# First loads in another order and in smaller pieces, and a last norm with other steps, in a one-core decoder layer

## The chip, the core and the metric

The kernel runs on one core of a Trainium2 chip. The metric is the device time of one execution in microseconds; three executions were timed and their median is given. One more execution was recorded by the hardware profiler. TensorE (PE) multiplies matrices, VectorE (DVE) and ScalarE (ACT) work on elements, GpSimd (POOL) too; loads and stores are issued from the queues of SyncE (SP), ScalarE and GpSimd and carried by 16 DMA engines.

## The reference

One layer of a hybrid decoder, over 512 prompt tokens and 8 x 8 sample tokens, 576 columns in all. Two branches, an RWKV-7 state scan and a differential attention, read the same normalised input; gates merge them, an MLP with squared ReLU follows, and a final RMSNorm.

```
def rmsnorm(x, g, eps):
    y = x * lax.rsqrt(jnp.mean(x * x, axis=-1, keepdims=True) + eps)
    return y * g

xn = rmsnorm(x, g_mix, 1e-6)
P = xn @ w_in                      # 1024 -> 1792 + 1536 + 2048 columns
o_a, S = rwkv7_branch(P[:1792], ...)
o_b = attend(q, k, v from P[1792:3328], ...)
m = sigmoid(P[3328:4352]) * (o_a @ w_br_a) + sigmoid(P[4352:]) * (o_b @ w_br_b)
x = x + m @ w_out
hn = rmsnorm(x, g_ffn, 1e-6)
x = x + square(relu(hn @ w_up)) @ w_down
y = rmsnorm(x, g_final, 1e-6)
```

All tensors are float32. The kernel lays features on the 128 partitions and tokens along the columns: x is eight tiles (k-tiles) of 128 features by 576 tokens.

## The kernel before

Every product of two float32 matrices is made of three products. An operand is split into a rounded high half and the rest (`hi` by ScalarE, line 58; `lo` by VectorE, line 61), and hi x hi, hi x lo and lo x hi are added up in one PSUM bank (`stream`, lines 158 to 201). A weight tile goes through three steps for that: load, `hi`, `lo`.

The kernel does not write the order of its instructions down. Each gets a priority (`prio`, a lower number is earlier), and a scheduler places the instructions of each engine by priority and by the time at which it thinks that their inputs are there. `FEED` is for loads and halves, `FILL` for matmuls; without either the place in the program counts. Eight semaphores serve the loads of SP's and ScalarE's queues in turn, so a load that takes one up again waits until the last transfer on it has landed.

The start: line 111 loads `vec`, all per-channel vectors (67 columns, 33.5 KB), and line 113 `cst`, the masks and the identity (374 KB), both from ScalarE's queue. Lines 275 to 291 load the eight tiles of x (288 KB each) and the first weights of q, k and v in pieces of four k-tiles (256 KB) from SP's queue. Then `xh` is x scaled by a column of `vec` and rounded, `xl` the rest (lines 297 and 298). The first norm's squares are summed beside it (`acc`), and its factor R1 is multiplied in later. `qkv(0)` multiplies the k-tiles for q, k and v in turn, each with two halves of 288 tokens. Nine products of a constant tile warm TensorE up (`warmup`).

The second norm (from line 1280): `colsum` sums the squares `acc` over the partitions on TensorE, one column a group of tokens; from it come M2 and R2 = 1/m, for the columns of all tokens. The MLP's input is not scaled by M2, so its result must be scaled: the residual is multiplied by M2 when the first product is added, and the last sum by R2.

The final norm: the last down products are made for 320 tokens first and 256 after (`LAST`). For each of the eight output tiles, `ev` adds the product to the residual (`fin`), scales it by R2, and squares it. The squares of seven tiles are added to `acc`; those of the last one are summed apart (`last`). Two column sums, one power (GpSimd, line 1351), and transposes that spread the factor over the partitions (`pb`) follow; ScalarE copies the factor to SBUF as R3 for GpSimd. VectorE multiplies six output tiles from the bank `pb`, GpSimd two (1 and 4) from R3, and four stores write them, ending after tiles 1, 3, 5 and 8 (`ends`), from SP and ScalarE in turn.

Of the kernel before, what the change touches and what calls it, by code (L numbers as in the profile page):

```python
# [8 lines left out]
F32 = mybir.dt.float32  # L9
# [6 lines left out]
P = 128  # L16
D = 1024
# [24 lines left out]
def tile_hybrid_step(ctx, tc, xT, xsT, ktab, vtab, s0T, ptab, w_in, vecs, w2a2, g2, lamv,  # L42
# [70 lines left out]
    nc.scalar.dma_start(out=c, in_=cst)  # L113
# [20 lines left out]
    def v(i, n=1):  # L134
        return vec[:, i:i + n]
# [18 lines left out]
    def stream(src, kt, xh, xl, spans, evac, name, raws=None, together=False, banks=None,  # L154
# [12 lines left out]

        def halve(i):
            raw = raws[i]
            with prio(FEED + 1000 * job + 100 if banks is None else FEED + 1001 + 40 * i + job):  # L170
                if keep:
                    hi, lo = (t[:, i * n:(i + 1) * n] for t in keep)
                elif banks is None or i == 0:
                    hi = ring["pool"].tile([P, n, P], F32R, tag="hi", name=f"hi_{name}_{i}")
                    lo = ring["pool"].tile([P, n, P], F32R, tag="lo", name=f"lo_{name}_{i}")
                else:
# [4 lines left out]
                his.extend(hi[:, k] for k in range(n))  # L181
                los.extend(lo[:, k] for k in range(n))
# [88 lines left out]
    with tc.tile_pool(name="xin", bufs=2, reuse_waits="tile") as xin:  # L271
        xt = [xin.tile([P, NT], F32, name=f"x{k}", bufs=1) for k in range(KT)]
        xs_ = xin.tile([P, KT, NB], F32, name="xs", bufs=1)
        acc = xin.tile([P, NT], F32, name="acc", bufs=1)
        with prio(FEED):
            nc.sync.dma_start(out=xt[0], in_=xT[:, 0])
        first = [(j + 1, []) for j in range(3)]
        for k in range(0, KT, 4):
            for j in range(3):
                with prio(FEED + 1000 + 10 * k + j):  # L280
                    name = f"raw_{'qkv'[j]}0_{k}"
                    if k == 0:
                        raw = ring["pool"].tile([P, 4, P], F32, tag="raw", name=name, bufs=3)
                    else:
                        raw = zw.tile([P, 1 + NX], F32, tag="z" if j else "tz", name=name,
                                      bufs=2 if j else 1)[:, :4 * P].rearrange("p (k w) -> p k w", k=4)
                    ring["dma"] = nc.sync.dma_start(out=raw, in_=w_in[14 + 4 * j][:, k:k + 4])
                    first[j][1].append(raw)
            with prio(FEED + 1005 + 10 * k):
                for i in range(max(k, 1), k + 4):  # L290
                    nc.sync.dma_start(out=xt[i], in_=xT[:, i])
# [3 lines left out]
        for k in range(KT):  # L295
            with prio(FEED + 1000 + 10 * k):
                act(xh[:, k, :NT], xt[k], scale=v(V_GM + k))
                stt(xl[:, k, :NT], xt[k], v(V_GM + k), f32(xh[:, k, :NT]), MUL, SUB)
# [869 lines left out]
    ends = (1, 3, 5, 8)  # L1168
# [5 lines left out]
    qs = {}  # L1174

# [308 lines left out]
```

## Time and profile before

| | |
|---|---|
| median of three executions | 1007.83 us (1004.7 to 1008.62) |
| the profiled execution | 1006.88 us, its span 1005.1 us |
| TensorE busy | 975.1 us, 97% of the span |
| VectorE, ScalarE, GpSimd busy | 688.9, 497.0, 87.5 us |
| DMA | 105.75 MB, 105 GB/s in the mean |

The span is what the profiler saw from the first instruction to the last; the execution's own time is 1.8 us more. Busy times overlap. The chain of waits follows the work that ended last back to its start, each time to what released it, and so shows which engine's time counts at which place.

### The profile page before, as it was taken

What the parts mean: (1) busy time and instruction counts of PE and PEld (TensorE: products, weight loads), DVE (VectorE), ACT (ScalarE), POOL (GpSimd) and SP (SyncE); (2) the same over time, 40 slices, a digit from 0 to 9 for tenths busy, and PEclk for the clock granted to TensorE, in tenths of its full rate; (3) what the DMA queues carried; (4) which work ended last, traced back from release to release, by engine and by line L of the source; (5) the groups of instructions that cost most, each with busy time, mean ns of one, the idle gap of its engine ahead of it and who ended that gap; (6) DMA issues with size and microseconds to landing.
All of it is one profiled execution on the core that took longest, in us unless ns stands there. A gap on an engine that the chain in (4) does not pass through costs nothing.

```text
span 1005.1 us, 24415 instructions
## 1 busy us (share of the span) xinstructions
PE 975.1 (97%) x10012; PEld 919.4 (91%) x10012; DVE 688.9 (69%) x1459; ACT 497.0 (49%) x1094; POOL 87.5 (9%) x171
## 2 busy tenths in 40 slices
PE   9999999899999998999989999999999999999996
PEld 9999998898887887988779999999999999999996
DVE  6698566864946679444579898966666666666644
ACT  6576455354435355453334666644444444444732
POOL 2511001301010340000210000000000000000001
PEclk9999999999989999999999999999999999999999
DMA  7422673211111234323357642222222222221402
GB/s 266 136 70 83 205 223 114 61 64 45 43 59 45 69 106 152 104 81 113 103 182 225 206 140 86 83 95 85 88 92 85 85 84 85 84 87 41 135 3 95
DMA packets 50833, 105.75 MB, mean 105 GB/s; under 512 B 6066, under 2 KB 8114, under 8 KB 50594
## 3 DMA queue, kind: packets, MB, share of 16 engines
q1 hardware_dynamic: 47442, 96.95, 30.4%
q0 software_dynamic: 1648, 5.35, 1.5%
q8 instruction: 79, 1.29, 0.5%
q10 hardware_dynamic: 1632, 1.89, 0.5%
q14 instruction: 32, 0.26, 0.1%
HBM read 89.38 MB, written 14.78 MB: 104 GB/s over the span
## 4 chain that ended last, share of the span: by engine, by line
PE 83%; DVE 6%; ACT 4%; issue 3%; DMA 2%; POOL 1%; SPq 0%; DVEq 0%; ACTq 0%; POOLq 0%
PE ps_dn L72 20%; PE ps_g L72 8%; PE ps_z L72 8%; PE ua L1220 5%; PE ux L1220 5%; PE ps_wo L72 4%; PE ps_k L72 3%; PE uc L1220 3%; PE ub L1220 3%; PE ud L1220 2%; PE ps_bra L72 2%; PE ps_q L72 2%; PE pch L72 2%; PE ps_brb L72 2%; PE ps_v L72 2%
## 5 line engine op out<-in xcount | busy, mean ns | idle before, releaser
L72 PE MATMUL ps_dn<-q,hi_dn 128*128 128x288 f32 x768 | 154.7, 296 | 0.0
L72 PEld LDWEIGHTS ps_dn<-q,hi_dn 128*128 128x128 f32 x768 | 122.7, 188 | 1.4
L72 PE MATMUL ps_dn<-q,lo_dn 128*128 128x288 f32 x384 | 113.2, 295 | 0.0
L72 PE MATMUL ps_g<-xl,hi_g 128*128 128x288 f32 x256 | 79.7, 311 | 0.0
L72 PE MATMUL ps_g<-xh,hi_g 128*128 128x288 f32 x256 | 79.0, 309 | 0.0
L72 PE MATMUL ps_g<-xh,lo_g 128*128 128x288 f32 x256 | 79.0, 309 | 0.0
L72 PEld LDWEIGHTS ps_dn<-q,lo_dn 128*128 128x128 f32 x384 | 72.0, 188 | 0.0
L72 PE MATMUL ps_z<-xh,lo_z 128*128 128x288 f32 (+1 forms) x224 | 68.9, 308 | 0.0
L72 PE MATMUL ps_z<-xh,hi_z 128*128 128x288 f32 (+1 forms) x224 | 67.6, 302 | 0.0
L72 PE MATMUL ps_z<-xl,hi_z 128*128 128x288 f32 (+1 forms) x224 | 66.8, 298 | 0.0
L61 DVE TENSOR_TENSOR ya<-ya,ps_dn 128x288 f32<-128x288 f32 x96 | 43.2, 451 | 29.4 <-PE ps_dn L72 29.4
L58 ACT ACTIVATE hi_dn<-raw_dn 128x512 fp32r<-128x512 f32 x48 | 30.1, 628 | 57.0 <-PE ps_dn L72 57.0
L1220 PE MATMUL ua<-h_b,hi 128*128 128x288 f32 x256 | 53.2, 298 | 0.0
L1220 PE MATMUL ux<-h_t,hi 128*128 128x288 f32 x256 | 52.3, 296 | 0.0
L58 ACT ACTIVATE c<-c 128x288 f32<-128x288 f32 x112 | 48.4, 439 | 7.4 <-DVE c L61 5.8
L72 PEld LDWEIGHTS ps_g<-xh,hi_g 128*128 128x128 f32 x256 | 48.7, 190 | 3.1 <-issue 1.8
L72 PEld LDWEIGHTS ps_g<-xl,hi_g 128*128 128x128 f32 x256 | 48.6, 190 | 1.9
L72 PEld LDWEIGHTS ps_g<-xh,lo_g 128*128 128x128 f32 x256 | 48.6, 190 | 1.6 <-DVE lo_g L61 0.2
L58 ACT ACTIVATE hi<-a 128x1024 fp32r<-128x1024 f32 (+1 forms) x32 | 27.1, 846 | 42.0 <-PE ps_dn L72 34.2
L72 PE MATMUL ps_dn<-q,w 128*128 128x320 f32 (+1 forms) x336 | 46.3, 297 | 0.0
L61 DVE TENSOR_TENSOR lo<-s,hi 128x1024 fp32r<-128x1024 f32 x32 | 39.2, 1224 | 10.1 <-ACT hi L58 10.0
L72 PEld LDWEIGHTS ps_dn<-q,w 128*128 128x128 f32 x336 | 45.3, 190 | 0.1
(395 smaller groups left out, 2802.2 us busy)
## 6 DMA issues: line engine op xcount, KB each, us to landing
a<-in_w_up_dram SPq DMA_DIRECT2D x32, 512.0 KB, 3.4
raw_dn<-in_w_down_dram SPq DMA_DIRECT2D x64, 256.0 KB, 2.8
raw_g<-in_w_in_dram SPq DMA_DIRECT2D x32, 256.0 KB, 3.1
raw_z<-in_w_in_dram SPq DMA_DIRECT2D x28, 256.0 KB, 3.1
gt_d<-gg SPq DMA_DIRECT2D x16, 288.0 KB, 2.4
g<-gt_d SPq DMA_DIRECT2D x16, 288.0 KB, 3.6
kp<-in_ktab_dram SPq DMA_DIRECT2D x16, 256.0 KB, 4.5
vp<-in_vtab_dram SPq DMA_DIRECT2D x16, 256.0 KB, 3.8
```

What stands on the lines that cost most here:

```text
L58: ring["act"] = AE.activation(out=out, in_=in_, func=func, **kw)
L61: ins = (eng or VE).tensor_tensor(out=out, in0=a, in1=b, op=op)
L72: ring["mm"] = PE.matmul(out=out, lhsT=lhsT, rhs=rhs, start=start, stop=stop)
L1220: ring["mm"] = PE.matmul(out=ps[:, :288], lhsT=l[:, k], rhs=hb[blk][:, h, k], start=start and i == 0, stop=i == 11, skip_group_check=skip)
```

## The change

At the start: the first tile of x is loaded as two halves of 288 tokens, and `xh` and `xl` of it are made in halves. The first weights of q, k and v come as one k-tile (64 KB, from ScalarE's queue) and three k-tiles (192 KB, from SP's), each with its own `hi` and `lo`. The constants move behind the last x on SP's queue. The second norm gets two more column sums, which put the sums of squares of the last 256 tokens in the two token groups that the last part has; from them VectorE makes r2b = 1/m squared. In the final norm, the last tile of the second part is squared before it is scaled, and its column sum is scaled by r2b instead. The factor is spread into two banks, `pb` for VectorE and `pb2` for ScalarE's copy; GpSimd multiplies tile 1 only, and there are five stores.

```
--- before.py
+++ after.py
@@ -110,7 +110,6 @@
     vec = const.tile([P, V_END], F32, name="vec")
     nc.scalar.dma_start(out=vec, in_=vecs)
     c = const.tile([P, C_END], F32, name="cst_sb")
-    nc.scalar.dma_start(out=c, in_=cst)
     ident = c[:, C_ID:C_ID + P]
     onesblk = c[:, C_OB:C_OB + P]
     ones1 = const.tile([P, 1], F32, name="ones1")
@@ -165,21 +164,28 @@
         else:
             job, raws = raws or load(src, kt, name)
 
+        if banks:
+            four = [ring["pool"].tile([P, n, P], F32R, tag=half, name=f"{half}_{name}_0") for half in ("hi", "lo")]
+
         def halve(i):
             raw = raws[i]
             with prio(FEED + 1000 * job + 100 if banks is None else FEED + 1001 + 40 * i + job):
+                m = n
                 if keep:
                     hi, lo = (t[:, i * n:(i + 1) * n] for t in keep)
-                elif banks is None or i == 0:
+                elif banks is None:
                     hi = ring["pool"].tile([P, n, P], F32R, tag="hi", name=f"hi_{name}_{i}")
                     lo = ring["pool"].tile([P, n, P], F32R, tag="lo", name=f"lo_{name}_{i}")
+                elif i < 2:
+                    m = 3 if i else 1
+                    hi, lo = (t[:, i:i + m] for t in four)
                 else:
                     hi, lo = (zp.tile([P, NT], F32R, tag=f"Pt{job - 1}", name=f"{half}_{name}_{i}", bufs=2)[
                         :, :n * P].rearrange("p (k w) -> p k w", k=n) for half in ("hi", "lo"))
                 act(hi, raw)
                 tt(lo, raw, f32(hi), SUB)
-                his.extend(hi[:, k] for k in range(n))
-                los.extend(lo[:, k] for k in range(n))
+                his.extend(hi[:, k] for k in range(m))
+                los.extend(lo[:, k] for k in range(m))
         for i in range(len(raws)):
             halve(i)
         pss = banks or [psd.tile([P, 512], F32, tag="d", name=f"ps_{name}_{i}") for i in range(len(spans))]
@@ -272,30 +278,42 @@
         xt = [xin.tile([P, NT], F32, name=f"x{k}", bufs=1) for k in range(KT)]
         xs_ = xin.tile([P, KT, NB], F32, name="xs", bufs=1)
         acc = xin.tile([P, NT], F32, name="acc", bufs=1)
+
+        first = [(j + 1, []) for j in range(3)]
+        raw0 = [ring["pool"].tile([P, 4, P], F32, tag="raw", name=f"raw_{'qkv'[j]}0_0", bufs=3) for j in range(3)]
         with prio(FEED):
-            nc.sync.dma_start(out=xt[0], in_=xT[:, 0])
-        first = [(j + 1, []) for j in range(3)]
-        for k in range(0, KT, 4):
+            for t0, n in HALF:
+                nc.sync.dma_start(out=xt[0][:, t0:t0 + n], in_=xT[:, 0, t0:t0 + n])
             for j in range(3):
-                with prio(FEED + 1000 + 10 * k + j):
-                    name = f"raw_{'qkv'[j]}0_{k}"
-                    if k == 0:
-                        raw = ring["pool"].tile([P, 4, P], F32, tag="raw", name=name, bufs=3)
-                    else:
-                        raw = zw.tile([P, 1 + NX], F32, tag="z" if j else "tz", name=name,
-                                      bufs=2 if j else 1)[:, :4 * P].rearrange("p (k w) -> p k w", k=4)
-                    ring["dma"] = nc.sync.dma_start(out=raw, in_=w_in[14 + 4 * j][:, k:k + 4])
-                    first[j][1].append(raw)
-            with prio(FEED + 1005 + 10 * k):
-                for i in range(max(k, 1), k + 4):
-                    nc.sync.dma_start(out=xt[i], in_=xT[:, i])
+                nc.scalar.dma_start(out=raw0[j][:, 0:1], in_=w_in[14 + 4 * j][:, 0:1])
+                first[j][1].append(raw0[j][:, 0:1])
+        with prio(FEED + 1):
+            nc.sync.dma_start(out=xt[1], in_=xT[:, 1])
+            for j in range(3):
+                nc.sync.dma_start(out=raw0[j][:, 1:4], in_=w_in[14 + 4 * j][:, 1:4])
+                first[j][1].append(raw0[j][:, 1:4])
+            for i in (2, 3):
+                nc.sync.dma_start(out=xt[i], in_=xT[:, i])
+        for j in range(3):
+            with prio(FEED + 1040 + j):
+                raw = zw.tile([P, 1 + NX], F32, tag="z" if j else "tz", name=f"raw_{'qkv'[j]}0_4",
+                              bufs=2 if j else 1)[:, :4 * P].rearrange("p (k w) -> p k w", k=4)
+                ring["dma"] = nc.sync.dma_start(out=raw, in_=w_in[14 + 4 * j][:, 4:8])
+                first[j][1].append(raw)
+        with prio(FEED + 1045):
+            for i in range(4, KT):
+                nc.sync.dma_start(out=xt[i], in_=xT[:, i])
+
+            nc.sync.dma_start(out=c, in_=cst)
         ring["job"] = 3
         with prio(FEED + 4000):
             nc.sync.dma_start(out=xs_, in_=xsT)
         for k in range(KT):
             with prio(FEED + 1000 + 10 * k):
-                act(xh[:, k, :NT], xt[k], scale=v(V_GM + k))
-                stt(xl[:, k, :NT], xt[k], v(V_GM + k), f32(xh[:, k, :NT]), MUL, SUB)
+                for t0, n in HALF if k == 0 else ((0, NT),):
+                    t = slice(t0, t0 + n)
+                    act(xh[:, k, t], xt[k][:, t], scale=v(V_GM + k))
+                    stt(xl[:, k, t], xt[k][:, t], v(V_GM + k), f32(xh[:, k, t]), MUL, SUB)
         for k in range(KT):
             if k == 0:
                 act(acc, xt[k], AF.Square)
@@ -1165,13 +1183,14 @@
 
 
     LAST = ((0, 320), (320, 256))
-    ends = (1, 3, 5, 8)
+    ends = (1, 3, 5, 7, 8)
 
 
     hq_pool = pool("hq", 8, stack=ctx, reuse_waits="tile")
     ft = pool("ft", 2, stack=ctx, reuse_waits="tile")
     ahead = []
     qs = {}
+    r2b = const.tile([P, 2], F32, name="r2b")
 
     def up_pair(f1):
 
@@ -1281,6 +1300,9 @@
 
                     pst = bank("pst2")
                     colsum(pst, acc, ones1, 1)
+                    for j in range(2):
+                        t = LAST[1][0] + j * P
+                        mm(pst[:, 5 + j:6 + j], acc[:, t:t + P], ones1)
                 with prio(FEED + 1000 * ring["job"]):
                     m2 = stat.tile([P, 5], F32, tag="r", name="m2")
                     r2 = stat.tile([P, 5], F32, tag="s", name="r2")
@@ -1288,6 +1310,11 @@
                     ts(m2[:, 0:4], pst[:, 0:4], 1.0 / D, MUL, 1e-6, ADD)
                     ts(m2[:64, 4:5], pst[:64, 4:5], 1.0 / D, MUL, 1e-6, ADD)
                     VE.reciprocal(out=r2, in_=m2)
+
+                    VE.tensor_copy(out=r2b, in_=pst[:, 5:7])
+                    ts(r2b, r2b, 1.0 / D, MUL, 1e-6, ADD)
+                    tt(r2b, r2b, r2b, MUL)
+                    VE.reciprocal(out=r2b, in_=r2b)
                 with prio(FILL + 1000 * ring["job"] + 1999):
                     spread(M2, m2, "M2")
                 with prio(FILL + 1000 * ring["job"] + 9999):
@@ -1315,6 +1342,13 @@
                 r = ft.tile([P, LAST[0][1]], F32, tag="c", name=f"fin{d}{t0}", bufs=4)
                 r = r[:, :n]
                 tt(r, ps, o, ADD)
+                if d == KT - 1 and t0:
+
+                    sq = ft.tile([P, LAST[0][1]], F32, tag="c", name="sqlast", bufs=4)[:, :n]
+                    act(sq, r, AF.Square)
+                    last.append(sq)
+                    tt(o, r, R2[:, span], MUL)
+                    return
                 tt(o, r, R2[:, span], MUL)
                 if d == 0:
                     act(acc[:, span], o, AF.Square)
@@ -1322,10 +1356,7 @@
                     sq = ft.tile([P, LAST[0][1]], F32, tag="c", name=f"sqf{d}{t0}", bufs=4)
                     sq = sq[:, :n]
                     act(sq, o, AF.Square)
-                    if d < KT - 1 or t0 == 0:
-                        tt(acc[:, span], acc[:, span], sq, ADD)
-                    else:
-                        last.append(sq)
+                    tt(acc[:, span], acc[:, span], sq, ADD)
             s_ = stream(None if t0 else w_down[3, d], KT, qh, ql, ((t0, n),), ev, f"dn3{d}_{t0}", keep=rows[d])
             finish(s_)
             ahead.append((ring["act"], ring["tt"]))
@@ -1345,7 +1376,8 @@
                 if i == 0:
                     ts(sums[:m, w], pst[:m, w], 1e-6, ADD)
                 else:
-                    tt(sums[:m, w], sums[:m, w], pst[:m, w], ADD)
+                    for j in range(w.start, w.stop):
+                        stt(sums[:, j:j + 1], pst[:, j:j + 1], r2b[:, j:j + 1], sums[:, j:j + 1], MUL, ADD)
         r3 = stat.tile([P, 5], F32, tag="r", name=f"r3{t0}")
         w = slice(0, len(tiles))
         GE.tensor_tensor(out=r3[:, w], in0=sums[:, w], in1=mhalf[:, w], op=ALU.pow)
@@ -1354,9 +1386,14 @@
             for j, (t, m) in enumerate(tiles):
                 tr(pb[:, t:t + m], bc(r3[:m, j:j + 1], [m, P]), ident[:m, :m])
         R3 = ft.tile([P, LAST[0][1]], F32, tag="R3", name=f"R3{t0}")
-        act(R3[:, :n], pb[:, :n])
+
+        pb2 = bank(f"pb4{t0}")
+        with prio(FILL + 1000 * ring["job"] + 4999):
+            for j, (t, m) in enumerate(tiles):
+                tr(pb2[:, t:t + m], bc(r3[:m, j:j + 1], [m, P]), ident[:m, :m])
+        act(R3[:, :n], pb2[:, :n])
         for d in range(KT):
-            if d in (1, 4):
+            if d == 1:
                 tt(ya[:, d, span], ya[:, d, span], R3[:, :n], MUL, GE)
             else:
                 tt(ya[:, d, span], ya[:, d, span], pb[:, :n], MUL)
```

The order of the instructions on ScalarE at the start, before (xh is x scaled by `vec`, hi and raw the weights; a wait on DMAHW is one on a load's semaphore, the others name engines):

```order
L111 DMA vec<-in_vecs_dram 128x67
L58 ACT_TABLE_LOAD
L58 ACTIVATE warm<-ones_77 128x1 [waits DVE_49]
L113 DMA cst_sb<-in_cst_dram 128x748
L58 ACTIVATE xh<-x_126,vec 128x576 [waits DMAHW1_49,DMAHW0_49]
L58 ACTIVATE hi_q_0_233<-raw_q_0_137 128x512 [waits DMAHW2_49]
L58 ACTIVATE hi_k_0_247<-raw_k_0_139 128x512 [waits DMAHW3_49]
L58 ACTIVATE acc<-x_126 128x576
L58 ACTIVATE hi_v_0_261<-raw_v_0_141 128x512 [waits DMAHW5_49]
```

And now, without the first two rows (the 64 KB load of raw_q and the load of ScalarE's function table):

```order
L58 ACTIVATE warm<-ones_76 128x1 [waits DVE_49]
L288 DMA raw_k_0_136<-in_w_in_dram 128x128
L288 DMA raw_v_0_137<-in_w_in_dram 128x128
L58 ACTIVATE hi_q_0_239<-raw_q_0_135 128x128 [waits DMAHW0_49]
L111 DMA vec<-in_vecs_dram 128x67 [waits DMAHW1_49]
L58 ACTIVATE acc<-x_125 128x576 [waits DMAHW3_49]
L58 ACTIVATE hi_k_0_255<-raw_k_0_136 128x128 [waits DMAHW5_49]
L58 ACTIVATE hi_q_0_239<-raw_q_0_135 128x384 [waits DMAHW4_49]
L58 ACTIVATE hi_v_0_271<-raw_v_0_137 128x128 [waits DMAHW6_49]
L58 ACTIVATE hi_k_0_255<-raw_k_0_136 128x384 [waits DMAHW7_49]
L58 ACTIVATE xh<-x_125,vec 128x288 [waits DMAHW1_49]
L58 ACTIVATE xh<-x_125,vec 128x288
```

The load of `vec` went from the first place to behind the first hi, and the first xh from the first real work to the eleventh row here, behind acc and five pieces of weights.

SP's queue at its start before, where x_126 is the first tile of x:

```order
L276 DMA x_126<-in_xT_dram 128x576
L287 DMA raw_q_0_137<-in_w_in_dram 128x512
L287 DMA raw_k_0_139<-in_w_in_dram 128x512
L287 DMA raw_v_0_141<-in_w_in_dram 128x512
L291 DMA x_127<-in_xT_dram 128x576
L291 DMA x_128<-in_xT_dram 128x576
L291 DMA x_129<-in_xT_dram 128x576 [waits DMAHW0_49]
L287 DMA raw_q_4_146<-in_w_in_dram 128x512 [waits DMAHW1_49]
```

And now, where x_125 is the first tile, in halves, and x_126 the second:

```order
L286 DMA x_125<-in_xT_dram 128x288
L291 DMA x_126<-in_xT_dram 128x576
L286 DMA x_125<-in_xT_dram 128x288
L293 DMA raw_q_0_135<-in_w_in_dram 128x384
L293 DMA raw_k_0_136<-in_w_in_dram 128x384
L293 DMA raw_v_0_137<-in_w_in_dram 128x384 [waits DMAHW0_49]
L296 DMA x_127<-in_xT_dram 128x576 [waits DMAHW2_49]
L296 DMA x_128<-in_xT_dram 128x576 [waits DMAHW3_49]
L301 DMA raw_q_4_149<-in_w_in_dram 128x512 [waits DMAHW4_49]
```

The second tile of x went between the halves of the first; the weights of q, k and v follow in pieces of 384 columns.

VectorE at the end of the program before, from the last product's addition (s is the sum, r the power, pb the spread factor):

```order
L61 TENSOR_TENSOR fin_13364<-ps_dn_320_0_13339,ya 128x256 [waits PE_49]
L69 TENSOR_SCALAR s_13370<-pst_13372 128x2 [waits PE_49]
L61 TENSOR_TENSOR ya<-fin_13364,R_8043 128x256 [waits DVE_49]
L61 TENSOR_TENSOR s_13370<-s_13370,pst_13376 128x2 [waits DVE_49,PE_49]
L61 TENSOR_TENSOR ya<-ya,pb_13382 128x256 [waits Activation_49]
L61 TENSOR_TENSOR ya<-ya,pb_13382 128x256 x5
```

And now:

```order
L61 TENSOR_TENSOR fin_13388<-ps_dn_320_0_13363,ya 128x256 [waits PE_49]
L69 TENSOR_SCALAR s_13394<-pst_13396 128x2 [waits PE_49]
L61 TENSOR_TENSOR ya<-fin_13388,R_8055 128x256 [waits DVE_49]
L66 SCALAR_TENSOR_TENSOR s_13394<-pst_13400,r2b,s_13394 128x1 [waits DVE_49,PE_49]
L66 SCALAR_TENSOR_TENSOR s_13394<-pst_13400,r2b,s_13394 128x1
L61 TENSOR_TENSOR ya<-ya,pb_13407 128x256 [waits PE_49]
L61 TENSOR_TENSOR ya<-ya,pb_13407 128x256 x4
L61 TENSOR_TENSOR ya<-ya,pb_13407 128x256 [waits Activation_49] x2
```

The add of the sums became two instructions, one a column, and the first multiplication waits for TensorE and no longer for ScalarE; only the last two wait for ScalarE, which scales their tiles by g_final.

## Rows read from the trace of the kernel before

**Rows 1.** The page's first part: busy time (us), share of the span, instructions.

```profile
PE 975.1 (97%) x10012; PEld 919.4 (91%) x10012; DVE 688.9 (69%) x1459; ACT 497.0 (49%) x1094; POOL 87.5 (9%) x171
```

**Rows 2.** Chain of waits, first 40 us: start us, us, what, count.

```profile
1.20 4.22 DMA raw_q<-in_w_in_dram
...
5.44 0.64 ACT hi_q L58
...
6.12 1.33 PE ps_q L72 x4
...
8.69 0.72 PE ps_k L72 x3
...
10.61 0.27 PE ps_v L72 x2
...
13.15 0.80 PE ps_q L72 x6
```

**Rows 3.** Timeline, first 14 us: start, us, engine, operation [idle before <- releaser].

```profile
0.74 0.41 ACTq L111 DMA_DIRECT2D vec<-in_vecs_dram  x1
...
1.12 4.21 PE L72 MATMUL warmup<-onesP 128*128 128x128 f32 x18 [1.12 <-DVE R L383]
...
4.23 0.78 ACT L58 ACTIVATE xh<-x,vec 128x576 fp32r<-128x576 f32 x1 [1.56 <-DMA vec<-in_vecs_dram]
...
6.44 0.63 ACT L58 ACTIVATE hi_k<-raw_k 128x512 fp32r<-128x512 f32 x1 [0.37 <-DMA raw_k<-in_w_in_dram]
```

**Rows 4.** Chain of waits, end of the span.

```profile
995.33 0.42 DVE fin L61
...
996.25 0.42 ACT sqf L58
...
996.72 0.62 PE pst L72 x4
...
997.36 0.17 DVE s L61
...
997.60 0.70 POOL r L1351
...
998.35 0.45 PE pb L76 x2
```

**Rows 5.** Stretch table: us, busy per engine, granted clock, DMA share, GB/s.

```profile
6.10:8.00 1.90, 1.88 (x7) 1.86 (x8) 1.44 (x2) 1.56 (x3) 0.20 (x2) 1.00 0.89 293
```

**Rows 6.** DMA rate in the first 14 us, 40 slices of 0.35 us.

```profile
GB/s 0 0 0 0 0 81 106 251 353 386 390 432 371 411 349 287 228 293 242 216 269 382 388 382 421 398 414 405 386 421 410 390 424 421 402 395 415 415 402 402
```

**Rows 7.** Timeline, end of the span.

```profile
998.82 0.38 ACT L58 ACTIVATE R<-pb 128x256 f32<-128x256 f32 x1 [1.61 <-PE pb L76]
999.24 2.07 DVE L61 TENSOR_TENSOR ya<-ya,pb 128x256 f32<-128x256 f32 x6 [1.71 <-ACT R L58]
999.28 1.41 POOL L61 TENSOR_TENSOR ya<-ya,R 128x256 f32<-128x256 f32 x2 [0.98 <-ACT R L58]
```

**Rows 8.** The page's fifth part: a ScalarE group of 288 columns.

```profile
L58 ACT ACTIVATE c<-c 128x288 f32<-128x288 f32 x112 | 48.4, 439 | 7.4 <-DVE c L61 5.8
```

**Rows 9.** DMA from 996 to 1006: rate in slices of 0.25 us; issues, us to landing.

```profile
GB/s 0 0 0 0 0 0 0 0 0 0 0 0 0 0 0 0 0 0 262 254 328 319 365 340 303 365 344 352 344 348 266 4 0 0 0 0 0 0 0 0
...
out_yT_dram<-ya ACTq DMA_DIRECT2D x1, 384.0 KB, 2.8
out_yT_dram<-ya ACTq DMA_DIRECT2D x1, 256.0 KB, 2.2
...
out_yT_dram<-ya SPq DMA_DIRECT2D x1, 128.0 KB, 1.8
```

**Rows 10.** Chain of waits from 600 to 620 us.

```profile
615.44 0.12 PE pst L72 x2
```

**Rows 11.** Chain of waits near 980 us.

```profile
980.30 0.11 PE pb L76
...
980.76 0.20 PE pb L76
```

## The prediction

> **What bounds the kernel now.** I read the engines' busy line first: TensorE is busy 97% of the span [rows 1], so only three kinds of time can change the end: what lies before its first real matmul, what lies after its last one, and instructions added to its own stream. The chain of waits of the first 40 us comes next [rows 2]: the load of the first query weights, issued at 1.20, lands at 5.42; ScalarE rounds it for 0.64 us (the high half, hi_q), and the first matmul starts at 6.12. From there the chain is TensorE alone. The timeline of the same stretch [rows 3] shows what stood beside it: the warm-up matmuls, which end at 5.33; the scale vector `vec`, issued at 0.74 and landed when xh starts at 4.23 (33.5 KB in 3.5 us); and the key weights, landed at 6.44. Last, the chain at the end [rows 4]: from the last product's addition at 995.33 every step waits for the one before: scaling, squaring, column sum, add, power, transpose, copy to SBUF (R), multiply, store. The span ends at 1005.1, so this tail is 9.8 us.
>
> TensorE starts at half speed. Three matmuls of 288 columns take 0.72 us in the chain at 8.69, that is 0.24 each, and six take 0.80 at 13.15, 0.133 each; the change comes at about 10.6 [rows 2]. 0.24 us is 288 columns at 1.2 GHz, 0.133 lies near 2.4. The granted clock's column says 1.00 in the slow stretch too [rows 5], so I go by the spacing.
>
> **The start.** Taken away: a 374 KB constant load beside the first loads, and the first matmul's wait for a whole 256 KB weight load. Added: the first weights come as 64 KB and 192 KB, x0 as two loads of 144 KB. What decides is where `vec` went. Every xh needs it as its scale. It was ScalarE's first instruction; now its DMA stands behind hi_q and waits for a queue semaphore that the first half of x0 releases. Behind it, in ScalarE's order and ahead of the first xh, stand the square of x0 (which needs the second half), hi_k, two more pieces of q and v, and the 384-column piece of hi_k. So the first matmul has two new gates.
>
> Gate one, ScalarE's order. The 384-column piece needs the second key load. On SP's queue 144 + 288 + 144 + 192 + 192 = 960 KB are moved until it is in, and on ScalarE's 3 x 64 + 33.5 = 225 KB: 1185 KB. Before, the key load was behind 800 KB on one queue (288 + 256 + 256, itself counted) and up to 407 KB on the other (vec, constants), 1207 KB, and landed at 6.44. The same bytes at the same rates [rows 6] give 6.4. The piece takes about 0.5 us (0.63 for 512 columns [rows 3], 0.38 for 256 [rows 7]), half an xh 0.44 [rows 8], then the matmul: 6.4 + 0.5 + 0.44 + 0.05 = 7.4.
>
> Gate two, `vec`. The half of x0, issued at 0.75, lands between 2.6 (after 1.8 us, as a 128 KB store [rows 9]) and 4.2 (vec's landing before). Vec then takes between 1.8 (the same store) and 3.5 (its own time) and lands between 4.4 and 7.7; nearest to its own rows, a little under, at about 6.8. That is below gate one's 6.9, so I take 7.4 for the first matmul, 1.3 us later than before, with ends at 6.4 (the key load lands at 5.42, as the query load did) and 8.2 (7.7 + 0.44 + 0.05): +0.3 to +2.1.
>
> On SP the last first-tile piece (v) waits for the first query piece to land, with x2 and x3 behind it. By 3.9 us some 550 KB had moved at the old rates [rows 6] of 1150 issued, so the engines don't run dry. After its start TensorE runs on: 18 matmuls of a k-tile take 2.4 us even at full speed, an xh 0.78 on ScalarE [rows 3]. The constants, now behind the last x, are first needed by transposes some 20 us later.
>
> How much of the 1.3 us stays depends on the slow stretch, 6.12 to 10.6, 19 matmuls. If the speed rises at the same moment, 5.3 fewer run slow, 5.3 x 0.107 = 0.6 comes back and +0.7 is left. If the stretch moves with the first matmul, all +1.3 stays. One execution does not show which; I take the middle, +1.0. The Trainium skill (TensorE: Matmul & The Clock Gate, Part 1) says that warm-up is an amount of time and not a number of matmuls, and that the monitor runs freely, not from a kernel's start; that alone would make the start's cost anything between the two, and no run here shows it.
>
> **The middle.** Two column sums of one column are added to the second norm's sum of squares. Such a sum costs 0.12 us in the chain at 615 us [rows 10], with no idle time of TensorE around it: +0.24. Four small VectorE instructions go with them, 0.17 or less each by the small sum of the tail's chain [rows 4]; TensorE waits for none, so 0, and 0.7 at most.
>
> In the first 320 tokens' norm the three transposes are made twice, for a second bank. The chain shows 0.11 for each of the first two and 0.20 for the last [rows 11], between matmuls that wait for nothing: +0.42.
>
> **The tail.** By the order on VectorE and ScalarE, step by step on the old clock. The last squares are now taken from the sum and not from the scaled one: they start when the addition ends, 995.79 instead of 996.25: -0.46. The small add of 0.17 becomes two instructions, +0.12 by their overlap with a neighbour. The transposes start at 998.0 (998.35 before). VectorE's first multiply now waits for the transposes alone, not for ScalarE's copy: 998.48 instead of 999.24. It has seven instead of six, spaced (2.07 - 0.42) / 5 = 0.33 [rows 7], and ends at 998.48 + 6 x 0.33 + 0.42 = 1000.88, against 1001.31. GpSimd has one multiply of 0.7 instead of two; with the second bank filled after the first, ScalarE's copy starts only 0.12 earlier, at 998.70, and GpSimd's row (until 999.9) holds the second group of the store.
>
> So the stores leave at about 998.94 (128 KB), 999.92 and 999.96 (256 each), 1000.6 (256) and 1000.9 (128); before, the last left after 1001.31 with 384 KB. What that is worth has two bounds. If each transfer has its own time, the last 384 KB took 2.8, 256 KB 2.2 and 128 KB 1.8 [rows 9]: the end comes at 1000.6 + 2.2 = 1002.8 instead of 1001.34 + 2.8, -1.35. If it is a matter of the rate, the engines are full at 300 to 365 GB/s from 1000.5 to 1003.65 [rows 9]; the second group can't come before 1000.75, and 896 KB at 340 then end at 1003.4: -0.25. The row shows no hole, so I stay near it: -0.5. The Trainium skill (DMA: Bandwidth & Descriptors, Anatomy of one DMA) gives each transfer about 2 us and its bytes over 436 GB/s, a fit for GpSimd's queue; by it the last store would need an estimated 2.3 instead of 2.9, the tail would give 1.0 and the sum be 0.5 lower. The 1.8 of the row is below that.
>
> **Sum.** +1.0 + 0.24 + 0.42 - 0.5 = +1.2 us on the profiled execution's 1006.88: 1008.1. That execution lies 0.95 under the median shown; on the median it would be 1009.0. I forecast 1008.6, midway (the midpoint before is 1007.4).
>
> **The rivals.**
> First: the start costs next to nothing and the tail gives its most. The key load lands early (+0.3), the speed rises when it did (0.3 x 0.133 / 0.24, +0.2), the store goes by the last transfer: +0.2 + 0.66 - 1.35 = -0.5, 1006.9. For it speak the lighter early loads, against it ScalarE's order.
>
> Second, slower: the idle time between the warm-up's end (5.33) and the first real matmul, 2.1 instead of 0.8 us, lets TensorE start colder, and its slow stretch lasts twice as long. 19 more matmuls at 0.107 extra cost 2.0: +1.3 + 2.0 + 0.66 - 0.25 = +3.7, 1011.1. It passes 5 us only if the stretch lasts until about 20 us (7.4 + 51 x 0.24). For it speaks that the warm-up did not lift the speed by 6.12 even with a gap of 0.8; against it that the first products follow without another gap.
>
> Third, faster: the loads in small pieces let TensorE go straight on from its warm-up at 5.4, at the speed that it otherwise has at 10.6: -0.7 - 2.0 + 0.66 - 1.35 = -3.4, 1004.0. The place of `vec` excludes it unless loads land over a microsecond earlier than any did before.
>
> Fourth, the new order in the second norm holds something up or frees it: its transposes stand two matmuls elsewhere. The chain there shows no wait, so 0.5 either way, 1008.1 or 1009.1.
>
> **How the numbers follow.** Forecast 0.55, first rival 0.22, second 0.13, third 0.04, fourth 0.06. A measurement tells about 0.5%, 5 us, from no change; runs of before alone spread from 1004.7 to 1008.6. No case by itself passes that bound; with the runs' spread, faster 0.05, same 0.88, slower 0.07. The range runs from 1006.9 less the 2.4 by which the lowest run lies under the mean of the three, to 1011.1 plus the 0.8 by which the highest lies over their median: 1004.5 to 1012.0.
>
> **What would show it.** Right: the first `ps_q` matmul at 7 to 8 us, released by an xh that waited for `vec` or for ScalarE's work on the second key load; three more transposes near 981; the last half's first multiply released by TensorE, 0.7 us nearer to the last product; a tail of 9 to 9.6 us. Wrong: a first matmul before 6.2, a speed change after 14 us, a tail under 8.5, or TensorE idle in the second norm.

## The result and the profile after

The changed kernel takes 1009.56 us (median of 15, 1006.73 to 1012.81), the kernel before 1005.2 us (median of 15, 1002.43 to 1008.62; two of the three runs known ahead are the two highest among them). The ratio is 1.0041, interval 1.0029 to 1.0053: 4.1 us slower (2.9 to 5.3), inside the 0.5% that was called no change but for the interval's upper end, and more than the 1.2 us forecast. The profiled execution takes 1008.65 us with a span of 1006.8, only 1.8 more than the one of before (1006.88): two single executions understate the difference here, and why is a part of the story.

The chain of waits of the changed kernel, first 40 us, which answers to [rows 2] (start, us, what):

```profile
1.67 4.07 DMA x<-in_xT_dram
...
5.75 0.68 ACT acc L58
6.44 0.20 ACT hi_k L58
6.64 0.41 ACT hi_q L58
7.05 0.20 ACT hi_v L58
7.25 0.41 ACT hi_k L58
7.66 0.50 ACT xh L58
...
8.20 0.61 PE ps_q L72
8.81 0.24 PE ps_k L72
...
10.97 0.54 PE ps_k L72 x3
...
12.18 0.79 PE ps_q L72 x6
...
28.87 0.99 PE pst L72 x10
```

The chain begins with a load of x, not of weights: the second half of x0, on SP's queue behind the whole of x1, lands at 5.73. ScalarE is then never idle: the square of x0, four pieces of weights, and at 7.66 the first xh. The first matmul starts at 8.20, 2.08 us later than before. It is slow again (0.24 us a matmul until about 11) and the first head's products end, where the column sum `pst` begins, at 28.87. Before, the same place was

```profile
27.48 0.99 PE pst L72 x10
```

so 1.4 us of the 2.08 arrive there. The timeline of the same stretch, for the other gate, answers to [rows 3]:

```profile
1.12 3.79 PE L72 MATMUL warmup<-onesP 128*128 128x128 f32 x18 [1.12 <-DVE R L401]
...
3.62 0.31 ACT L58 ACTIVATE hi_q<-raw_q 128x128 fp32r<-128x128 f32 x1 [0.92 <-DMA raw_q<-in_w_in_dram]
3.62 0.35 ACTq L111 DMA_DIRECT2D vec<-in_vecs_dram  x1
...
7.67 0.26 POOL L69 TENSOR_SCALAR mu<-vec 128x14 f32<-128x14 f32 x1 [4.93 <-DMA vec<-in_vecs_dram]
```

`vec` is issued at 3.62, not at 0.74, and GpSimd's first use of it, which waits for nothing else, starts at 7.67: 4.0 us for 33.5 KB among the loads of SP's queue. Both gates open within 0.1 us of each other.

The stretches of the same time (us, busy of TensorE, its weight loads, VectorE, ScalarE, GpSimd, granted clock, DMA share, GB/s), which answer to [rows 5]:

```profile
5.00:8.20 3.20, 0.00 (x0) 0.00 (x0) 1.41 (x4) 2.44 (x7) 0.53 (x2) 0.93 1.02 314
8.20:11.00 2.80, 2.80 (x11) 2.80 (x12) 2.70 (x6) 2.79 (x5) 2.77 (x7) 0.50 0.89 260
11.00:14.00 3.00, 3.00 (x24) 3.00 (x23) 2.19 (x4) 1.50 (x3) 0.63 (x1) 0.97 0.96 349
```

TensorE is idle from 4.9 to 8.2. Here the clock's column shows a fall within that gap, 0.50 (1.2 GHz) in the first 2.8 us of real products, and a return by 14 us (at about 11.2). The nine warm-up products (18 matmuls in the trace) took 3.79 us instead of 4.21: in this profile the speed had come up in the warm-up and was lost in the gap.

The chain at the end answers to [rows 4] and [rows 11]:

```profile
984.58 0.11 PE pb L76
...
985.03 0.20 PE pb L76
...
996.73 0.44 DVE fin L61
...
997.19 0.42 ACT sqlast L58
...
997.66 0.62 PE pst L72 x4
...
998.30 0.36 DVE s L66 x2
...
998.79 0.71 POOL r L1383
...
999.54 0.45 PE pb L76 x2
...
1000.01 0.42 DVE ya L61
```

The second set of three transposes stands at 984.58 to 985.23: 0.11 + 0.11 + 0.20, as expected. In the tail the squares start 0.46 after the addition instead of 0.92, the power at 2.06 instead of 2.27, the first multiplication at 3.28 instead of 3.91. Yet the span ends 10.07 us after the addition started, against 9.77 before. The DMA rate from that addition on, in slices of 0.25 us, and two of the three groups of stores (KB each, us to landing), which answer to [rows 9]:

```profile
GB/s 0 0 0 0 0 0 0 0 0 0 0 0 0 0 0 0 0 0 217 295 12 0 131 360 344 332 303 369 336 348 340 360 340 107 0 0 0 0 0 0
...
out_yT_dram<-ya ACTq DMA_DIRECT2D x2, 256.0 KB, 3.3
out_yT_dram<-ya SPq DMA_DIRECT2D x2, 128.0 KB, 2.4
```

The first store moves its 128 KB in the slices from 4.5 to 5.0, then the engines stand still for half a microsecond, and run full until 8.4. Before, they ran without a hole from about 5.2 to 8.5. The earlier start was used up by the hole, and 256 KB from ScalarE's queue now land after 3.3 us (the median of two) instead of 2.2. The span also ends later behind the last byte: 1.6 us, against 1.3 before.

### The profile page after: what moved, and what is told of

It reads as the page before. It is cut to its first block, busy times and chain, and to the rows that moved or that the text cites. A ratio compares the mean times of both kernels' runs of the same rounds, so it can differ in the third digit from the quotient of the medians.

```text
span 1006.8 us, 24458 instructions
## 1 busy us (share of the span) xinstructions
PE 974.7 (97%) x10021; PEld 919.3 (91%) x10021; DVE 690.7 (69%) x1470; ACT 498.0 (49%) x1098; POOL 86.9 (9%) x169
## 4 chain that ended last, share of the span: by engine, by line
PE 83%; DVE 6%; ACT 4%; issue 3%; POOL 2%; DMA 1%; SPq 0%; DVEq 0%; POOLq 0%; ACTq 0%
PE ps_dn L72 20%; PE ps_g L72 9%; PE ps_z L72 8%; PE ua L1239 5%; PE ux L1239 5%; PE ps_wo L72 4%; PE uc L1239 3%; PE ps_k L72 3%; PE ps_bra L72 2%; PE ub L1239 2%; PE ud L1239 2%; PE ps_q L72 2%; PE pch L72 2%; PE ps_v L72 2%; PE pA L72 2%
```

## The experiments

One table for all, read from the chains and the timelines (us): the first real matmul; the gap that TensorE was idle between its warm-up and that matmul; the time until which a matmul of 288 columns took 0.24 us and not 0.13 (a dash: the products run fast from the start); the end of the first head's products; the tail (from the last addition to the end of the span); and the ratio to the kernel before with its interval. Each row but the ratio is one execution. The us over before that stand below are the ratio and its interval, taken of 1005 us.

| kernel | first matmul | gap | slow until | head ends | tail | ratio |
|---|---|---|---|---|---|---|
| before | 6.12 | 0.8 | 10.5 | 27.48 | 9.77 | |
| changed | 8.20 | 3.3 | 11.2 | 28.87 | 10.07 | 1.0041 (1.0029 to 1.0053) |
| changed, again | 8.14 | 2.8 | 13.3 | 29.79 | 10.12 | 1.0031 (1.0019 to 1.0044) |
| start_only | 8.05 | 2.7 | 14.0 | 30.07 | 9.97 | 1.0044 (1.0029 to 1.0060) |
| norm_only | 6.37 | 1.2 | - | 26.53 | 10.36 | 1.0024 (1.0011 to 1.0038) |
| vec_first | 6.62 | 1.3 | 10.1 | 27.51 | 10.21 | 1.0012 (0.9999 to 1.0025) |
| warm18 | 8.11 | 0.1 | - | 27.49 | 10.30 | 1.0029 (1.0017 to 1.0040) |
| acc_late | 8.06 | 2.7 | 13.7 | 29.94 | 10.25 | 1.0045 (1.0028 to 1.0063) |
| alldve | 6.48 | 1.6 | - | 26.48 | 9.79 | 1.0016 (1.0004 to 1.0027) |
| gp_row4 | 6.43 | 1.1 | - | 26.76 | 9.87 | 1.0016 (1.0004 to 1.0028) |
| cst_last | 6.16 | 1.0 | - | 26.32 | 9.73 | 0.9998 (0.9987 to 1.0009) |
| best1 | 5.87 | none | - | 26.01 | 9.99 | 1.0012 (0.9997 to 1.0028) |
| best2 | 6.20 | 0.9 | - | 26.34 | 9.84 | 1.0013 (0.9998 to 1.0027) |

**start_only**: the start's edits without the norms'. Against the changed kernel:

```
-    ends = (1, 3, 5, 7, 8)
+    ends = (1, 3, 5, 8)
...
-            if d == 1:
+            if d in (1, 4):
```

> The start's edits alone (x0 in halves, first weights in pieces, constants last), the norms as before. Theory S (the start costs nearly all: vec stands behind hi_q, the first matmul comes at 8.2 and not at 6.1, and after an idle time of over 3 us TensorE runs at half speed again): first real matmul at 8.0 to 8.4, first head's products end 1.2 to 3 us later than before, time 3 to 4 us over before. Theory N (the norms cost most: five more small TensorE instructions, a longer tail): 0.5 to 1.5 us over before. Theory C (half-speed stretches that fall here and there in the middle make the difference by chance): no difference, within 1 us.

Measured 4.4 us over before (2.9 to 6.0). Its chain:

```profile
8.05 0.61 PE ps_q L72
8.65 0.24 PE ps_k L72
...
30.07 0.99 PE pst L72 x10
```

The first matmul is where the changed kernel has it, but the head ends 1.2 us later still: 2.6 us behind the profile of before. Theory S holds for the start's part.

**norm_only**: the norms' edits without the start's, which is left as it was. Against the kernel before, two of the edits:

```
-    ends = (1, 3, 5, 8)
+    ends = (1, 3, 5, 7, 8)
...
-            if d in (1, 4):
+            if d == 1:
...
```

> The norms' edits alone, the start as before. Theory S: 0.3 to 1.2 us over before (0.24 + 0.42 for the added TensorE work, a tail from 0.3 longer to 0.5 shorter). Theory N: 2.5 to 4 us over before. Theory C: within 1 us. In the trace the span's end should come 9.6 to 10.2 us after the last product's addition starts, as in the changed kernel (10.1), against 9.8 before.

Measured 2.4 us over (1.1 to 3.8), with the tail at 10.36: between the two theories. Added work (0.66) and tail (0.3 to 0.6) make up 1.0 to 1.3; the interval reaches down to that, so whether more is there is open. The two parts add to 6.8 where the whole is 4.1; their intervals allow 4.0 to 9.8 together, so the split is known only roughly. The chain of its start, which is the start of before, shows something else:

```profile
8.46 0.78 ACT xh L58
...
9.28 0.40 PE ps_q L72
...
26.53 0.99 PE pst L72 x10
```

Here TensorE had its speed soon enough to run ahead of the loads: it waited for the second tile's xh until 9.28, and still ended the head 0.95 us earlier than the profile of before, which had been slow until 10.5. The later profiles with this start (alldve, gp_row4, cst_last, best2) are like this one: that of before was not typical.

**vec_first**: the changed kernel with the load of `vec` first.

```
-    nc.scalar.dma_start(out=vec, in_=vecs)
+    with prio(FEED - 1):
+        nc.scalar.dma_start(out=vec, in_=vecs)
```

> The changed kernel with the load of vec put first on ScalarE's queue again; everything else as changed. Theory S: the first real matmul comes at 5.0 to 6.5 instead of 8.2, and the time falls to between 1 us under and 1.5 us over before. Theory N: still 2.5 to 4 over before. If only the order of vec is to blame and not the rest of the start, the first head's products end no later than before (27.5).

Measured 1.2 us over before (-0.1 to 2.5), some 2.9 under the changed kernel (2.9 to 5.3 over before: the intervals don't overlap; against its second measurement, 1.9 to 4.4, they just do). The scheduler, which now expects `vec` early, also put the xh of x0 ahead of the weights on ScalarE: the first half's starts at 3.46, the second's waits for its half of x0 until 5.83, and hi_q, behind it, ends just before the first matmul at 6.62:

```profile
5.83 0.54 ACT xh L58
6.37 0.21 ACT hi_q L58
...
6.62 1.81 PE ps_q L72 x6
```

So the place of `vec`, with the order that the scheduler makes of it, is most of the cost. The rest of the new start (x0 and the first weights in pieces) gives nothing in this order: the first matmul is no earlier than the 6.1 to 6.5 of the old start. The first half's xh had ended at 4.00 and hi_q's 64 KB had landed at 4.67, so hi_q ahead of the second half's xh might gain; that was not tried. (This profile, 1008.8 us, is the slowest of the run's twelve executions.)

**warm18**: the changed kernel with more warm-up.

```
-        for _ in range(9):
+        for _ in range(18):
```

> The changed kernel with 18 warm-up products instead of 9, so that TensorE works until about 7 to 8.7 us; vec stays late. If the late first matmul alone costs: time as the changed kernel, 3.5 to 5 over before, first matmul at 8.2 to 9. If the half-speed stretch after the idle time is a part of the cost: no or a shorter stretch at 0.24 us a matmul behind the first, the first head's products end 1 to 1.5 us earlier than in the changed kernel (30.0 becomes 28.5 to 29), 2 to 3.5 over before.

Measured 2.9 us over (1.7 to 4.0). Its chain:

```profile
8.11 0.40 PE ps_q L72
8.51 0.14 PE ps_k L72
...
27.49 0.99 PE pst L72 x10
```

The first matmul is as late as in the changed kernel, and the products behind it run at 0.13 to 0.15 us each. The head ends 1.4 to 2.6 us earlier than in the four profiles that have the same late first matmul and 9 products (29.7 in their mean), and 0.8 later than the old start's mean with 9 products (26.7). So the late matmul costs in two ways, the delay itself and a slower TensorE behind the gap, and of the 3.0 us by which the head ends later the second is the larger part, about 2.2. This rests on one profile; the total time, 2.9 us over where the changed kernel has 4.1 and 3.1, does not tell warm18 from it.

**after_again**: the changed kernel, unchanged.

> The changed kernel once more, for a second profile of it. If the half-speed stretch behind the late first matmul comes from the idle time before it, it is there again, of a length that differs from run to run (2.9 us in the first profile): first head's products end 28 to 30.5, time 3 to 5 us over before. If the first profile was a chance: no stretch at half speed, head ends at 27.

Measured 3.1 us over (1.9 to 4.4; the medians, 1009.66 and 1005.32, differ by 4.3). The slow stretch lasts longer than in the first profile, and the warm-up before it took 4.21 us, slow to its end; six matmuls at 12.83 still take 1.06 us instead of 0.80:

```profile
12.83 1.06 PE ps_q L72 x6
...
29.79 0.99 PE pst L72 x10
```

**acc_late**: all squares of x behind the first xh.

```
+                    x0h = ring["act"] if k == 0 else x0h
...
-                act(acc, xt[k], AF.Square)
+                with tc.issue_after(x0h.ins):
+                    act(acc, xt[k], AF.Square)
```

(and the same for the seven other squares)

> The changed kernel with all squares of x moved behind the first xh on ScalarE, so that the pieces of weights need not wait for the square of x0. If the landing of vec (7.6 in the changed kernel) is the gate: first matmul at 8.0 to 8.4 again, ScalarE idle before the first xh. If ScalarE's order is the gate: first matmul at 6.9 to 7.7. Time 2.5 to 4.5 us over before by the first, 1.5 to 3.5 by the second.

Measured 4.5 us over (2.8 to 6.3, five executions), first matmul at 8.06. Timeline of ScalarE, its queue and GpSimd:

```profile
4.15 0.34 ACTq L111 DMA_DIRECT2D vec<-in_vecs_dram  x1
...
6.27 0.52 ACT L58 ACTIVATE hi_q<-raw_q 128x384 fp32r<-128x384 f32 x1 [1.43 <-DMA raw_q<-in_w_in_dram]
...
6.90 0.51 ACT L58 ACTIVATE hi_k<-raw_k 128x384 fp32r<-128x384 f32 x1
...
7.47 1.63 ACT L58 ACTIVATE xh<-x,vec 128x288 fp32r<-128x288 f32 x3
...
7.54 0.61 POOL L69 TENSOR_SCALAR mu<-vec 128x14 f32<-128x14 f32 x1 [4.80 <-DMA vec<-in_vecs_dram]
```

Without the square, hi_k still ends only at 7.41, since ScalarE waits until 6.27 for the 192 KB of hi_q that stand before it, and `vec`, issued at 4.15, is there at about 7.45: by 0.04 us it is the later here. In the four profiles that have the late `vec` and the square in its place, the changed kernel's two, start_only and warm18, ScalarE's pieces end last, 0.1 to 0.3 us after `vec` has landed. The two gates lie on each other: moving one away can't help.

**alldve**: the kernel before with the norms' edits and all last multiplications by VectorE. Against norm_only:

```
-        R3 = ft.tile([P, LAST[0][1]], F32, tag="R3", name=f"R3{t0}")
-        pb2 = bank(f"pb4{t0}")
...
         for d in range(KT):
-            if d == 1:
-                tt(ya[:, d, span], ya[:, d, span], R3[:, :n], MUL, GE)
-            else:
-                tt(ya[:, d, span], ya[:, d, span], pb[:, :n], MUL)
+            tt(ya[:, d, span], ya[:, d, span], pb[:, :n], MUL)
```

> The start as before; of the norms' edits the early last squares and the five stores stay, but VectorE makes all eight last multiplications from the one bank: no second bank, no second set of transposes, no copy R3, nothing for GpSimd. If the tail's gain was lost because the second store waits for GpSimd's tile (which waits for the second bank and ScalarE's copy): the DMA rate shows no hole behind the first store, the drain ends 0.4 to 0.8 earlier after the last product than in the changed kernel (8.3 us after the last addition starts), the span 9.2 to 9.8 after it instead of 10.1 to 10.4, and the time is -0.8 to +0.8 of before. Rival (the drain goes by its rate and by what comes after it, whoever multiplies): end at 10.0 to 10.4 again, time +0.5 to +2 over before.

Measured 1.6 us over (0.4 to 2.7), tail 9.79. The DMA rate from the last addition on:

```profile
GB/s 0 0 0 0 0 0 0 0 0 0 0 0 0 0 0 0 0 0 233 283 8 266 336 328 361 311 356 348 365 332 328 320 21 0 0 0 0 0 0 0
```

The hole is one slice instead of two, and the drain ends at about 8.1 instead of 8.4. The hole theory holds for its part, 0.3 us; but the end comes 1.6 us after the last byte, against 1.3 before, so the tail is only back where it was, and the time is over the range that the theory gave.

**gp_row4**: the kernel before with the norms' edits, GpSimd on tile 4. Against norm_only:

```
-            if d == 1:
+            if d == 4:
```

> As the norms' edits alone, but GpSimd has tile 4 instead of tile 1, so that the second store (tiles 1 and 2) needs VectorE only and the third waits for GpSimd. Hole theory: the hole of half a microsecond in the DMA rate is gone or smaller, the drain ends 0.2 to 0.6 earlier, span end 9.6 to 10.0 after the last addition. Rival: no change, 10.1 to 10.4.

Measured 1.6 us over (0.4 to 2.8), tail 9.87:

```profile
GB/s 0 0 0 0 0 0 0 0 0 0 0 0 0 0 0 0 0 0 127 348 49 160 324 356 332 328 360 348 344 344 328 352 94 0 0 0 0 0 0 0
```

The hole is filled but for one slice, the drain ends 0.25 earlier. Both kernels name the same cause of the hole: tile 1 was the tile not to give to GpSimd.

**cst_last**: only the constants moved.

```
-    nc.scalar.dma_start(out=c, in_=cst)
...
+        with prio(FEED + 1046):
+            nc.sync.dma_start(out=c, in_=cst)
```

> The kernel before with one part of the start's edit: the constants leave ScalarE's queue and come late on SP's; vec stays first, x and the first weights stay whole, norms as before. If the lighter queue brings the first weights earlier: first matmul at 5.5 to 6.2 (6.1 to 6.4 in the kernels with the old start), time -1 to 0 of before. If the constants cost nothing there: within 0.5 us. It should not be slower by 1 or more, as the changed start is.

Measured 0.2 us under before (1.3 under to 0.9 over): no difference. The first matmul comes at 6.16; the constants were no obstacle.

**best1** and **best2**: cst_last with the tail of alldve; best1 with 11 warm-up products, best2 with 9 and four stores. The line

```
-        for _ in range(9):
+        for _ in range(11):
```

is best1's, and best2's

```
-    ends = (1, 3, 5, 7, 8)
+    ends = (1, 3, 5, 8)
```

> Old start with the constants late, 11 warm-up products instead of 9 (so that TensorE has no idle time before its first real matmul), and the tail of alldve. If the speed reached in the warm-up is kept when no gap follows, and the tail gains: first head's products end at 26 to 27 (27.5 in the profile of before, 26.5 in that of the norms' edits alone), time 1 to 2.5 us under before. Rival (the start is bound by the loads of x anyway): -0.5 to +0.5 of before.

> Old start with the constants late (9 warm-up products), the early last squares, all last multiplications on VectorE from one bank, four stores. If a fifth store lengthens the end behind the drain (1.6 to 1.9 us from the last byte to the end of the span with five stores, 1.3 to 1.6 with four), the tail is 9.2 to 9.6 us against 9.7 to 10.0 with four stores and GpSimd, and 9.8 to 10.0 with five without it; time -1.5 to +0.3 of before. Rival: tail 9.8 again.

Measured 1.2 over (-0.3 to 2.8) and 1.3 over (-0.2 to 2.7): neither beats the kernel before. The head ends earliest of all in best1 (26.01), but 0.3 to 0.5 us are lost among the runs' scatter. The tail of best2, 9.84, looks like the rival's "9.8 again", but another thing lies in it. The last transposes of alldve, best1 and best2:

```profile
996.01 0.45 PE pb L76 x2
...
996.02 0.70 PE pb L76 x2
...
995.47 0.70 PE pb L76 x2
```

In best1 and best2 the granted clock had fallen to 0.50 before the transposes were through, which cost 0.25 us; in alldve it had not. Against best1, which shares that, four stores end the tail 0.15 us earlier than five (9.84 against 9.99). From the last byte to the end of the span it is 1.3 us in best2, as in the kernel before and cst_last, which have four stores too (1.5 in start_only, the fourth); in all nine profiles with five stores it is 1.6 to 1.9. So a fifth store does go with a later end, by some 0.3 us; the times of best1 and best2 can't show so little, and why it does was not looked for.

## Why the prediction was right, and where it was not

The direction of the sum and its place within 0.5% were right; its size was a third of the 4.1 us measured. That the forecast time, 1008.6, came near 1009.56 is luck: the 1007.4 that it started from lies 2.2 us above the larger sample's median.

*The two gates.* Right as a mechanism, with the place and the order as described; both sizes were too small. Gate one was priced by the landing of the second key piece, put at 6.4. It lands at 6.8 (issued at 2.62, 4.2 us), but ScalarE does not wait for it: what holds ScalarE is the second half of x0, which lands at 5.73, then its square until 6.44 and four pieces of weights until 7.66, all named, none of them priced. `vec` was put at 6.8 and landed at 7.6, near the upper bound of 7.7. The first matmul came at 8.05 to 8.20 in five profiles, the upper end of the range given (8.2) and not 7.4, and just past the 7 to 8 us that were to be the sign of being right.

*The slow stretch.* This is the mis-sized term. +1.0 was taken, midway between a speed that rises at the same moment and a stretch that moves along. Both took the slow stretch of the profile of before for the rule (its length was put at 19 matmuls; the chain has 17). It is not: in the other five profiles with the old start and 9 products the first products run fast at once, after gaps of 0.9 to 1.6 us. In all four with the new start, `vec` late and 9 products they run slow, for 3.0 to 5.9 us, after gaps of 2.7 to 3.3 us; with 18 products and no gap they run fast. That is the side of the second rival, the idle time before the first product. How it comes about is not the same in the four: in the first profile the speed had come up in the warm-up and fell in the gap, in the three others the warm-up was slow to its end. And the gap's length alone does not decide, for before ran slow after 0.8 us and vec_first after 1.3. In the mean over profiles the head ends at 29.7 with the new start (28.87, 29.79, 30.07, 29.94) and at 26.7 with the old one and 9 products (27.48, 26.53, 26.48, 26.76, 26.32, 26.34): +3.0 us, where the two profiles that the forecast could compare give +1.4. The one profile of before was the slowest of its kind; its clock column, at 1.00 through a slow stretch, was no help.

*The added TensorE work.* 0.42 for the transposes is there in the chain. Over the whole MLP, from the second norm's sums to the last addition, TensorE is busy for 379.9 us in the changed kernel and 379.2 before: 0.7 more, as the 0.66 says. But the time that passes is 380.0 us (both profiles) against 379.9, because TensorE was idle for 0.7 us between 942 and 946 us before, behind a load of weights (in its chain at 936.84, 4.3 us) and ScalarE's work on it, and for 0.1 us at that place in the changed kernel. The prediction took the work as added to the time; in this pair 0.1 of it is. With the old norms the time is 378.9, 379.9 and 380.0 in three profiles, with the new ones and both sets of transposes 379.9 to 380.5 in seven: +0.5 in the mean.

*The tail.* Every step up to the first multiplication came as worked out (-0.63 instead of -0.76). The bound by the rate was the right one, and -0.25 was its optimistic reading: the last byte is through 0.1 us earlier than before, no more. What had no term is that the end follows the last byte later with five stores (1.6 to 1.9 us against 1.3). Term: -0.5 forecast, +0.3 measured (10.07 to 10.36 against 9.73 to 9.97 with the old tail), outside the 9 to 9.6 us that were to be the sign of being right. In warm18, 0.25 of it is the slow clock at the transposes, as in best1 and best2.

*The rivals.* The first (a start for next to nothing) fell; the third fell; the fourth shows nothing above the scatter. The second was priced at +3.7 and is close to what the start and the tail cost together, 3.0 + 0.3. Its condition held, but not its reckoning: the stretch did not double (3.0 to 5.9 us, 4.4 in the profile of before), the old start mostly has none. That its number fits is in part chance.

Start, tail and added work make 3.0 + 0.3 + 0.1 = 3.4 us of 4.1 (2.9 to 5.3), or 3.8 with the mean of 0.5 for the work. The rest is within the interval and not placed.

## What to carry to other kernels

Before cutting first loads into pieces, look where the scheduler then puts the smallest load that everything needs: 33.5 KB that slid behind two waits cost more than any weights. A warm-up was worth its time here where the real work followed it closely; if the first inputs come later, try a longer one. And a first short store helps only if the second is ready when it is through: give the slow engine a tile of the last groups, not of the second, and set against it that one store more goes with an end some 0.3 us later.

## What the runs showed of the hardware that was not expected

With the old start and 9 products, TensorE ran its first products at 2.4 GHz in five profiles of six, after gaps of 0.9 to 1.6 us. In two of these (gp_row4, best2) the warm-up itself had been slow to its end, and the granted clock rose in the gap (at 5.8 and 5.4 us). With the new start and gaps of 2.7 to 3.3 us all four ran at 1.2 GHz; 2.4 GHz then came back at 11.2, 13.3, 13.7 and 14.0, that is 3.0 to 5.9 us after the first product. Gaps of 0.8 (before) and 1.3 us (vec_first) were followed by slow products too, so the gap alone does not tell.

The same falls occur in the middle. In the changed kernel two stretches of 5 us (us, busy, granted clock third from the end) were

```profile
245.00:250.00 5.00, 5.00 (x48) 3.96 (x48) 1.67 (x3) 3.82 (x8) 3.51 (x6) 0.67 0.17 57
385.00:390.00 5.00, 4.58 (x62) 4.09 (x66) 4.58 (x9) 2.15 (x4) 0.00 (x0) 0.66 0.82 241
```

and in the profile of before 275 to 285 and 510 to 515 (0.64 to 0.73). One fall, which begins at 275 to 281 us, stands in all thirteen profiles, the changed kernel's too, though not equally long; the others come in some and not in others. The time between the first head's end and the second norm, whose code no experiment touched, went from 585.8 to 589.4 us over the profiles. Effects under 2 us can't be read from a pair of profiles of this kernel; the medians of many runs were needed.

A load of 33.5 KB that was issued at 3.6 to 4.2 us, while another queue was full, took 3.2 to 4.0 us to land; issued first, at 0.74, it took 2.3 to 3.5, as against 1.8 us for a 128 KB store at the end of the kernel [rows 9].
